# A diffusion backbone on one core: a new issue order for its state-space layer, and the discretisation's factor moved from B into the powers

## The chip, the core and the metric

The program runs on one core of a Trainium2 chip. The core has a matrix engine (TensorE, PE in the profile; PEld is its weight load), three engines for elementwise work (VectorE = DVE, ScalarE = ACT, GpSimd = POOL), a queue engine for transfers (SyncE = SP), and 16 DMA engines. Each engine takes its own instructions strictly in the order in which the program issues them, and waits on semaphores for the others. The metric is device time in microseconds; lower is better.

## The reference

Two layers over 256 latent tokens of width 2048. Layer 0 mixes tokens with a bidirectional diagonal state-space layer over 128 groups of 16 channels and 64 states, followed by a GLU; layer 1 mixes with a pooling mixer. Each layer ends with a gated convolutional FFN. Norms, shifts, scales and gates come from a conditioning vector through a large weight `ada_w`. The part that the change touches:

```python
def _s5_discretize(lam_re, lam_im, log_step, b_re, b_im):
    dt = exp(log_step)[:, None]
    mag = exp(lam_re * dt)
    abar_re, abar_im = mag * cos(lam_im * dt), mag * sin(lam_im * dt)
    nr, ni = abar_re - 1.0, abar_im
    den = lam_re * lam_re + lam_im * lam_im
    fr = (nr * lam_re + ni * lam_im) / den
    fi = (ni * lam_re - nr * lam_im) / den
    bbar_re = fr[..., None] * b_re - fi[..., None] * b_im
    bbar_im = fr[..., None] * b_im + fi[..., None] * b_re

# per direction: h[t] = abar * h[t-1] + bbar u[t], first over 256 context tokens,
# then over the 256 latent tokens; y = Re(C h) + D u, and out = GLU(gelu(y) @ glu_w)
```

## The kernel before

The first 405 us of the program are the state-space layer; the GLU, the FFNs and the pooling mixer follow. The layer's tokens are cut into chunks of 8; the work inside a chunk goes through matrices made of powers of abar times B and C, and what passes from chunk to chunk goes through a tree and a scan. The groups are handled in two halves h of 64 groups, and these in eight blocks b of 8 groups.

The order of all instructions of this layer is one string, ORDER (line 30). Every name in it stands for a function; most functions are generators, and each mention runs one step of one, `*n` runs n steps. A step is a handful of instructions on one or two engines. The names that matter below:

- d1, d2, d3: the discretisation (`disc1` to `disc3`, lines 450 to 483): exponent, sine and cosine, and the factor (bbar = factor times B), kept in `fr` in three combinations. pl and ph add the position table to the tokens; sc, sx and s2 give the norms' factors (squares on ScalarE, sums on TensorE).
- b0, b1, b2 (`bbar`, line 485): seven VectorE steps each that multiply B by the factor, complex times complex with three products. b0 and b1 cover 32 groups each of half 0 (512 elements per partition), b2 all 64 of half 1 (1024 elements). B lies in `Bb`, three parts: the difference or sum, real, imaginary.
- p0, p1 (`powers`, line 504): powers 1 to 8 of abar, with difference and sum. qb (`q_b`, line 526) copies powers 0 to 7 for the B side on ScalarE, one direction forward, one backward; qo copies powers 1 to 8 for the C side; qa squares the eighth for the tree.
- B, T, S of a block, as B13 for half 1, block 3: B (`b_ops`) is five VectorE steps of 1024 elements that form powers times B, with a small GpSimd-queue load `Cz`; T (`b_turn`) has three parts: two halves that TensorE transposes and ScalarE copies, and a third ("lg") of small products with C, copied to a lag table, on which GpSimd runs two small additions; S (`s_unit`) multiplies the tokens with the transposed result on TensorE and copies it to the chunk states on ScalarE.
- t0 to t3 (`tree`) and Z0, Z1 (`scan`, 31 steps) run on VectorE alone. t0 needs S00 to S03, t1 S04 to S07, Z0 both; t2, t3, Z1 likewise in half 1.
- c loads C of a block on the GpSimd queue; C (`c_ops`) forms C times powers on VectorE in three steps; M (`m_turn`) transposes the lag table; H (`hist`) copies the scan's states on ScalarE and adds on GpSimd; Y (`y_unit`) is the block's output on TensorE, and needs C, M and H. O (`y_out`) is gelu, transposition and a split into two 16-bit halves for four blocks.
- k (`columns`) takes the shift and scale of a quarter of the columns from `mod`, through TensorE and ScalarE, to `ck`; D (`modulate`), u, in form the normalised, modulated tokens on VectorE.
- F (`feed`, line 213) loads 1 MB of `ada_w` on the SP queue into one of the slots st and multiplies it on TensorE; when a part of the columns is full, the next F or N (`finish`) takes the sums through ScalarE, TensorE and ScalarE again, and a GpSimd addition puts them into `mod`. "-" and "+" take slot 2 away and give it back.
- lB, lc, lx, lt, le are loads for half 1 (lB on SP, the others on the GpSimd queue). W, h, l, G start the GLU: weights loaded, their 16-bit high part (ScalarE), low part (VectorE), and the first products.

Buffers are shared: the scratch G, cut into `e[0]` to `e[5]`, Z and WH carry in turn B's products, the transposed blocks and C's products (`o_view`, three buffers for eight blocks). B of block b+2 writes where T's third part of block b reads; C of block b+3 writes where Y of block b reads.

Of the kernel before, what the change touches and what calls it, by code (L numbers as in the profile page):

```python
# [7 lines left out]
OP = mybir.AluOpType  # L8
# [3 lines left out]
P = 128  # L12
# [3 lines left out]
HG = 64  # L16
# [11 lines left out]


ORDER = """  # L30
d1*17 d2*39 sc pl ph F sx F*2 d3 b0 p0 b0 p0 b0*3 p0*2 b0*2 qb0 B00*5 F*2 N F*4 d2 s2 u0*2 k0 qo0 - T00*2 B02 T00 u1*2
D000 D001 D000 D001 B01*5 b1*7 S00*2 B02*4 F*2 T01*3 qa0 F*2 T02*3 B03*5 F S01*2 B04*5 F T03 F*2 S02*2 N k1 c01 T03*2
D010 D011 D010 D011 B05 S03*2 c00 T04*2 B05*4 B06 F B06 T04 B06*3 F S04*2 t0*2 T05*3 B07*5 S05*2 c02 F C00*3 c03 T06*3
S06*2 T07*3 F S07 t0*2 S07 C01*3 c04 t0*6 F t1*10 Z0 C02 lB lc lt le C02 Z0 lx Z0 C02 Z0 F c05 Z0 b2 Z0*4 b2 F b2 F Z0
F b2 Z0 b2 Z0 F*2 b2 M00 b2 Z0 F Z0 p1 Z0 F p1 Z0 F M01 p1 in Z0 in Z0 M02 F in Z0*3 p1 Z0*8 F Z0*2 F qb1 qa1 H00 H01
Y00*2 M03 H02 F C03*3 c06 k2 Y01 c07 Y01 H03 M04 F*2 C04*3 N k3 D101 D111 D101 Y02*2 H04 C05*3 Y03*2 D100 O0 M05 H05
M06 F C06*3 O0 Y04*2 H06 M07 + C07*3 qo1 D100 Y05*2 F H07 O0 Y06*2 B10*5 Y07*2 O1 F B11*5 - T10*2 D111 T10 T11*3 B12*5
S10*2 O1*2 D110*2 B13*5 F S11 T12*3 B14*4 S12*2 F T13*3 B15*3 S11 B14 F T14*2 B15*2 F S13*2 c10 C10 F C10*2 T14 F B16
T15*3 B16*4 S14*2 c11 t2*2 B17*5 S15*2 c12 t2*6 F t2*2 c13 T16*3 S16*2 T17*3 S17*2 C11*3 c14 F C12 F*2 t3*4 F t3*5 t3
Z1 C12 Z1*2 F C12 Z1 c15 Z1*5 F Z1*2 M10 F Z1*4 M11 Z1 Z1 F Z1*2 M12 Z1*2 F Z1 F Z1*3 F*2 Z1*2 F Z1*4 H10 H11 Y10*2 H12  # L40
M13 C13*3 c16 Y11*2 H13 M14 Y12 F Y12 H14 M15 C14 C15*2 Y13 C15 Y13 C14*2 c17 O2 H15 M16 C16*2 F C16 Y14*2 H16 O2 M17 F
C17*3 Y15*2 F N W*3 H17 h O2 Y16*2 Y17*2 l O3*2 G O3
"""


class Net:
# [331 lines left out]
    def s5(self):  # L378
        tc, nc, A = self.tc, self.nc, self.A
        con, par = self.con, self.par  # L380
        with tc.tile_pool(name="s5c", bufs=1) as cp, tc.tile_pool(name="tb", bufs=2) as tb, tc.tile_pool(
# [63 lines left out]
            w = e[2][:, 0:1024].rearrange("p (v g) -> p v g", v=8)  # L445
# [20 lines left out]
            def disc3():  # L466
                self.mul(ab, ab, mg[:, None, :].to_broadcast([P, 2, NG]))
                nr, t1, t2 = w[:, 0], w[:, 1], w[:, 3]
                self.ts(nr, ab[:, 0], -1.0, OP.add)
                self.mul(t1, lr, lr)  # L470
                self.mul(t2, li, li)
                self.mul(w[:, 5], nr, lr)
                self.add(t1, t1, t2)
                self.mul(w[:, 6], ab[:, 1], li)
                nc.vector.reciprocal(w[:, 4], t1)
                self.mul(t1, ab[:, 1], lr)
                self.mul(t2, nr, li)
# [45 lines left out]

            pview = lambda mem: mem.rearrange("p (v k g) -> p v k g", v=4, k=8)

            def q_b(QB, pw):
                for lo, s in ((0, 7), (64, 0)):
                    nc.gpsimd.memset(QB[lo : lo + 64, 0, s], 0.0)
                    nc.gpsimd.memset(QB[lo : lo + 64, 1:3, s], 1.0)
                self.copy(QB[0:64, :, 0:7], pw[0:64, 1:4, 6::-1])  # L530
                self.copy(QB[64:128, :, 1:8], pw[64:128, 1:4, 0:7])

            def q_o(pw):
                self.copy(QO[0:64], pw[0:64, 1:4])
                self.copy(QO[64:128], pw[64:128, 1:4, ::-1])
# [261 lines left out]
            def st(v):  # L797
                sts[v] = stats((cx, xr)[v], v)

            ops = {  # L800
                "F": lambda: self.feed(1),
                "N": self.finish,
                "W": self.load,
                "h": lambda: self.high(0),
                "l": lambda: self.ensure(0),
                "G": self.glu0,
                "lB": lambda: nc.sync.dma_start(Bb[:, 1:3], A["b"][1]),
                "lc": lambda: nc.gpsimd.dma_start(rc, A["cck"][:, HG:, :]),
# [23 lines left out]
                ops[f"t{i}"] = lambda i=i: tree(32 * (i % 2), 32 * (i % 2) + 32)  # L832
            for h in range(2):
                ops[f"p{h}"] = lambda h=h: powers(h, pw[h])
                ops[f"qb{h}"] = lambda h=h: q_b(QB[h], pw[h])
                ops[f"qa{h}"] = lambda h=h: q_a(pw[h])
                ops[f"qo{h}"] = lambda h=h: q_o(pw[h])
                ops[f"Z{h}"] = scan
                for v in range(2):
                    for j in range(2):  # L840
                        ops[f"D{h}{j}{v}"] = lambda h=h, j=j, v=v: modulate(h, j, v)
                for b in range(8):
                    n = f"{h}{b}"
                    ops["B" + n] = lambda h=h, b=b: b_ops(h, b, QB[h], Bk[h][b], bm[h][b])
                    ops["T" + n] = lambda h=h, b=b: b_turn(h, b)
                    ops["S" + n] = lambda h=h, b=b: s_unit(h, b, bm[h][b])
                    ops["c" + n] = lambda h=h, b=b: c_load(h, b)
                    ops["C" + n] = lambda h=h, b=b: c_ops(h, b)
                    ops["M" + n] = lambda h=h, b=b: m_turn(h, b)
                    ops["H" + n] = lambda h=h, b=b: hist(b)  # L850
                    ops["Y" + n] = lambda h=h, b=b: y_unit(h, b)
            live = {}
            steps = (s.split("*") for s in ORDER.split())
            for tok in (s[0] for s in steps for _ in range(int(s[1]) if len(s) > 1 else 1)):
# [4 lines left out]
                r = ops[tok]()  # L859
# [601 lines left out]
```

## Time and profile before

| | us |
|---|---|
| median of 3 runs | 2081.57 (2080.56 to 2083.05) |
| profiled execution, device time | 2081.02 |
| its span, first to last instruction | 2079.2 |
| TensorE busy in the span | 1907.9 (92%) |
| VectorE busy | 1687.5 (81%) |
| ScalarE busy | 977.4 (47%) |
| GpSimd busy | 111.6 (5%) |

The page's strip of 40 equal slices shows two programs in one: in the first eight slices VectorE is at 7 to 9 tenths and TensorE goes up and down between 3 and 7; from the ninth slice on TensorE is at 9 tenths or more almost throughout, with one dip between the GLU and the first FFN and one at the pooling mixer. The page's chain of work that ended last reaches back only into the second part (PE 47% of the span), so the first part is read from the busy times by stage, the waits and the timelines. In those views a row of a wait names the waiting engine, what it wrote, and which engine ended the wait.

### The profile page before, as it was taken

The page shows a single profiled execution, that of the slowest core. Times are in us where ns is not written, and L with a number is a line of the kernel's source. Part 1 is how long each engine was busy: PE and PEld are TensorE (multiplying, and loading weights), DVE is VectorE, ACT ScalarE, POOL GpSimd, SP SyncE. Part 2 cuts the span into 40 slices and gives each one's busy share as a digit, 9 for nine tenths or more (in the row PEclk, how much of TensorE's full clock was granted, in tenths as well). Part 3 has the DMA queues.
Part 4 walks back from the last instruction along what each step waited for, and adds up shares of the span by engine and source line. Part 5 has one row for each costly group of instructions (what it writes and reads, how often), then busy time and mean ns, then how long its engine had stood idle before and what let it go on. Part 6 is the DMA issues. An engine that isn't in the chain of part 4 may idle for free. (4 is left out here: it accounts for less than half of the span.)

```text
span 2079.2 us, 44155 instructions
## 1 busy us (share of the span) xinstructions
PE 1907.9 (92%) x19300; PEld 1624.0 (78%) x19300; DVE 1687.5 (81%) x2204; ACT 977.4 (47%) x1139; POOL 111.6 (5%) x129
## 2 busy tenths in 40 slices
PE   5773775799989999999999999889999999999998
PEld 3651552688878888888888888578888888888886
DVE  8799889699889999999998898878777766654444
ACT  2341651655555554554444443655545555543442
POOL 0440251200000000000000000000000000000000
PEclk9785897899989999999999999889999999999999
DMA  8565347599938999999999999327767656555652
GB/s 320 223 237 215 138 179 264 217 356 367 334 111 335 340 355 341 333 338 328 343 332 357 358 366 353 137 100 264 259 236 261 242 201 203 198 190 201 209 201 77
DMA packets 77585, 541.62 MB, mean 260 GB/s; under 512 B 8912, under 2 KB 9168, under 8 KB 16464
## 3 DMA queue, kind: packets, MB, share of 16 engines
q1 hardware_dynamic: 74304, 526.06, 69.1%
q0 software_dynamic: 3088, 12.74, 1.6%
q8 instruction: 151, 2.47, 0.5%
q14 instruction: 42, 0.34, 0.0%
HBM read 536.67 MB, written 2.10 MB: 259 GB/s over the span
## 5 line engine op out<-in xcount | busy, mean ns | idle before, releaser
L82 PEld LDWEIGHTS <-WH 128*128 128x128 f16 x9472 | 927.3, 98 | 118.7 <-issue 9.5
L70 DVE SCALAR_TENSOR_TENSOR XW<-st,WH 128x2048 f16<-128x2048 f32 (+1 forms) x303 | 676.2, 2233 | 276.3 <-ACT WH L74 275.8
L74 ACT ACTIVATE WH<-st 128x2048 f16<-128x2048 f32 (+1 forms) x304 | 566.7, 1865 | 704.8 <-PE pu L82 364.4
L82 PE MATMUL pu<-Z,WH 128*128 128x256 f16 x5376 | 881.2, 273 | 0.0
L82 PE MATMUL pu<-Z,XW 128*128 128x256 f16 x2688 | 732.7, 273 | 0.0
L82 PEld LDWEIGHTS <-XW 128*128 128x128 f16 x4720 | 462.6, 98 | 59.6 <-issue 3.4
L82 PE MATMUL pd<-G,WH 128*128 128x256 f16 x2816 | 461.8, 273 | 0.2 <-DVE G L52 0.2
L82 PE MATMUL pd<-G,XW 128*128 128x256 f16 x1408 | 383.8, 273 | 0.0
L70 DVE SCALAR_TENSOR_TENSOR gac<-ra,cpad,gac 128x1024 f32<-128x1024 f32 x128 | 163.9, 1280 | 3.2 <-DMA ra<-ada 1.8
L82 PE MATMUL pg<-Z,WH 128*128 128x256 f16 x960 | 157.5, 273 | 0.0
L70 DVE SCALAR_TENSOR_TENSOR gac<-st,cpad,gac 128x1024 f32<-128x1024 f32 x112 | 143.4, 1281 | 7.3 <-DMA st<-ada 5.8
L70 DVE SCALAR_TENSOR_TENSOR hc<-pu,cvs,hc 128x255 f32<-128x255 f32 x336 | 138.6, 475 | 0.6 <-ACT hc L76 0.6
L82 PE MATMUL pg<-Z,XW 128*128 128x256 f16 x480 | 130.8, 273 | 1.6 <-DVE XW L70 1.6
L82 PE MATMUL gv<-st,cpad 128*32 128x128 f32 (+2 forms) x1024 | 87.7, 476 | 45.4 <-DMA st<-ada 45.4
L82 PEld LDWEIGHTS gv<-st,cpad 128*32 128x32 f32 x1024 | 30.9, 128 | 76.5 <-DMA st<-ada 60.7
L76 ACT ACTIVATE hc<-pu,par,cvs 128x256 f32<-128x256 f32 x168 | 84.3, 551 | 8.0 <-DVE G L52 8.0
L82 PE MATMUL y<-G,QX 128*32 128x128 f32 x768 | 32.0, 302 | 39.1 <-ACT QX L74 37.9
L82 PEld LDWEIGHTS y<-G,QX 128*32 128x32 f32 x768 | 23.9, 122 | 42.5 <-ACT QX L74 39.4
L52 DVE TENSOR_TENSOR G<-G,q 128x768 f32<-128x768 f32 (+2 forms) x56 | 49.8, 890 | 5.5 <-ACT q L74 3.6
L74 ACT ACTIVATE QX<-XW 64x512 f32<-64x512 f32 x32 | 35.7, 1116 | 36.3 <-DVE XW L52 30.3
L82 PE MATMUL pf<-Z,WH 128*128 128x256 f16 x256 | 47.7, 291 | 5.4 <-ACT Z L74 3.2
L74 ACT ACTIVATE hc<-hc 128x256 f32<-128x256 f32 x88 | 35.6, 405 | 27.7 <-DVE hc L70 26.4
(231 smaller groups left out, 1511.9 us busy)
## 6 DMA issues: line engine op xcount, KB each, us to landing
st<-up SPq DMA_DIRECT2D x176, 1024.0 KB, 6.2
st<-ada SPq DMA_DIRECT2D x128, 1024.0 KB, 6.8
ra<-ada SPq DMA_DIRECT2D x64, 1024.0 KB, 7.2
st<-down SPq DMA_DIRECT2D x64, 1024.0 KB, 5.1
st<-glu SPq DMA_DIRECT2D x32, 1024.0 KB, 7.5
st<-down SPq DMA_DIRECT2D x32, 768.0 KB, 5.3
Cz<-cz POOLq DMA_DIRECT2D x16, 256.0 KB, 5.3
G<-pool SPq DMA_DIRECT2D x4, 1024.0 KB, 8.5
```

Of the source, the lines that this page charges most:

```text
L52: self.nc.vector.tensor_tensor(out=out, in0=a, in1=b, op=op)
L70: self.nc.vector.scalar_tensor_tensor(out, a, s, b, op0, op1)
L74: self.nc.scalar.activation(out, a, f, scale=scale)
L76: self.nc.scalar.activation(out, a, f, bias=bias, scale=scale)
L82: self.nc.tensor.matmul(out, l, r, start=start, stop=stop)
```

## The change

Three functions change, and the order string is replaced as a whole.

- `bbar` becomes `bdiff`, one step: only the difference of B's parts is formed, without the factor.
- A new function `fpowers` (names f0, f1, seven steps each) multiplies powers 1 to 7 by the factor, 448 elements per step and partition; power 0 times the factor is a ScalarE copy of `fr`. Its result lies in QO for half 0 and in QX for half 1.
- `q_b` copies that result whole, 1536 elements for 1344, and its four GpSimd memsets per half go. `disc3` forms the three combinations of the factor with other signs, again in three instructions.

```diff
-d1*17 d2*39 sc pl ph F sx F*2 d3 b0 p0 b0 p0 b0*3 p0*2 b0*2 qb0 B00*5 F*2 N F*4 d2 s2 u0*2 k0 qo0 - T00*2 B02 T00 u1*2
-D000 D001 D000 D001 B01*5 b1*7 S00*2 B02*4 F*2 T01*3 qa0 F*2 T02*3 B03*5 F S01*2 B04*5 F T03 F*2 S02*2 N k1 c01 T03*2
-D010 D011 D010 D011 B05 S03*2 c00 T04*2 B05*4 B06 F B06 T04 B06*3 F S04*2 t0*2 T05*3 B07*5 S05*2 c02 F C00*3 c03 T06*3
-S06*2 T07*3 F S07 t0*2 S07 C01*3 c04 t0*6 F t1*10 Z0 C02 lB lc lt le C02 Z0 lx Z0 C02 Z0 F c05 Z0 b2 Z0*4 b2 F b2 F Z0
-F b2 Z0 b2 Z0 F*2 b2 M00 b2 Z0 F Z0 p1 Z0 F p1 Z0 F M01 p1 in Z0 in Z0 M02 F in Z0*3 p1 Z0*8 F Z0*2 F qb1 qa1 H00 H01
-Y00*2 M03 H02 F C03*3 c06 k2 Y01 c07 Y01 H03 M04 F*2 C04*3 N k3 D101 D111 D101 Y02*2 H04 C05*3 Y03*2 D100 O0 M05 H05
-M06 F C06*3 O0 Y04*2 H06 M07 + C07*3 qo1 D100 Y05*2 F H07 O0 Y06*2 B10*5 Y07*2 O1 F B11*5 - T10*2 D111 T10 T11*3 B12*5
-S10*2 O1*2 D110*2 B13*5 F S11 T12*3 B14*4 S12*2 F T13*3 B15*3 S11 B14 F T14*2 B15*2 F S13*2 c10 C10 F C10*2 T14 F B16
-T15*3 B16*4 S14*2 c11 t2*2 B17*5 S15*2 c12 t2*6 F t2*2 c13 T16*3 S16*2 T17*3 S17*2 C11*3 c14 F C12 F*2 t3*4 F t3*5 t3
-Z1 C12 Z1*2 F C12 Z1 c15 Z1*5 F Z1*2 M10 F Z1*4 M11 Z1 Z1 F Z1*2 M12 Z1*2 F Z1 F Z1*3 F*2 Z1*2 F Z1*4 H10 H11 Y10*2 H12
-M13 C13*3 c16 Y11*2 H13 M14 Y12 F Y12 H14 M15 C14 C15*2 Y13 C15 Y13 C14*2 c17 O2 H15 M16 C16*2 F C16 Y14*2 H16 O2 M17 F
-C17*3 Y15*2 F N W*3 H17 h O2 Y16*2 Y17*2 l O3*2 G O3
+d1 sc d1*2 lt d1*12 c00 d1*2 d2*8 c01 d2*17 c03 d2*2 pl d2*8 ph sx d3 p0 F*2 b1 p0 b0 p0*2 f0*7 qb0 qo0 s2 F*3 N B00*2
+u1 B01*2 B00*3 F B01 u0 B01*2 T00*2 F T01 u1 F*2 - T00 B02 T01*2 qa0 k0 d2 F*2 u0 B02*4 T02 D001 D000 T02*2 D001 D000
+S01*2 S00 B03*4 S00 B03 T03 B04*3 F T03*2 S02 F B05*4 S02 B05 B04*2 S03*2 F T04*2 F T04 B06*3 T05 B06*2 t0*2 T06 F*2 N
+T05*2 B07*3 t0 B07*2 k1 T07 t0 T07 d2 C00 D011 F D010 D011 T06 D010 S04*2 C00 t0*2 S07 lB d2 b2 t0*2 p1 S07 C00 p1*2
+t0 S06*2 lc p1 f1*4 S05 t0 S05 f1 t1*8 d2 F*2 M03 M00 c02 F*3 t1*2 Z0 T07 Z0*8 f1 F Z0*3 F*2 f1 qb1 Z0*10 M02 Z0 le
+M01 Z0 lx F Z0*4 M04 Z0 F Z0*2 T06 F*3 C01*3 H00 Y00 C02 c04 H01 Y00 H02 F Y01*2 H03 C03 C02*2 Y02 C03 in c05 Y02
+C04*3 F H04 M05 C03 Y03*2 F in O0 k2 c07 C05 c06 in C05*2 D101 H05 M07 F C06*2 Y04 C06 Y04 C07*2 c11 H06 M06 Y05*2 B10
+F*2 B10*3 O0 Y06*2 H07 N k3 C07 qo1 D100 Y07 O0 F B10 T10 D101 Y07 D100 O1 qa1 T10 + F T10 B11*4 D110 S10*2 O1 B11 F
+O1 B12*4 T11 - F B12 T11*2 S11*2 B13*5 T12 F D110 T12*2 T13 B14*3 S12*2 B14*2 T13 D111 F T13 B15*2 S13 B15*2 S13 T14 F
+T14*2 B15 T15*2 D111 B16*3 F B16*2 T15 S15 S14 B17*5 t2 S15 t2*7 S14 F t2*2 T16 F T16 T17*2 S16*2 S17*2 t3*7 F t3 F
+t3*2 M12 Z1*13 M14 F Z1 F*2 Z1*4 M13 c12 Z1*3 F Z1*4 F*2 T17 Z1 M11 Z1 F*3 Z1*4 M10 c10 C10*3 C11*3 T16 C12*2 d2 F*2
+C12 H10 Y10*2 H11 c13 c14 F H12 M15 c15 Y11 F Y11 H13 M16 Y12*2 H14 M17 C13*3 Y13*2 c16 C14*3 C15*3 C16*3 O2 F*2 W*3
+c17 Y14*2 H15 N C17 Y15*2 H16 Y16*2 C17*2 H17 Y17*2 h O3 O2 l O2 O3 G O3
@@ disc3
-                self.mul(fr[:, 0], t1, w[:, 4])
-                self.sub(fr[:, 1], w[:, 5], fr[:, 0])
-                self.stt(fr[:, 2], w[:, 5], -1.0, fr[:, 0], OP.mult, OP.subtract)
+                self.stt(fr[:, 0], t1, -1.0, w[:, 4], OP.mult, OP.mult)
+                self.add(fr[:, 1], fr[:, 0], w[:, 5])
+                self.sub(fr[:, 2], fr[:, 0], w[:, 5])
@@ bbar becomes bdiff; fpowers is new
-                self.sub(b[:, 0], b[:, 1], b[:, 2])
-                self.mul(v(1), v(1), f(1))
-                self.mul(v(2), v(2), f(2))
-                self.mul(v(0), v(0), f(0))
-                self.add(b[:, 1], b[:, 1], b[:, 0])
-                self.sub(b[:, 2], b[:, 2], b[:, 0])
-                self.add(b[:, 0], b[:, 1], b[:, 2])
+                self.sub(b[:, 0], b[:, 2], b[:, 1])
+            def fpowers(h, pw, pf):
+                m, p = pf[:, :, 1:8], pw[:, :, 0:7]
+                f = lambda r: fr[:, r, h * HG : (h + 1) * HG][:, None, :].to_broadcast([P, 7, HG])
+                self.copy(pf[:, :, 0], fr[:, :, h * HG : (h + 1) * HG])
+                self.mul(m[:, 2], p[:, 2], f(0))
+                self.mul(m[:, 1], p[:, 0], f(1))
+                self.mul(m[:, 0], p[:, 1], f(2))
+                self.sub(m[:, 1], m[:, 1], m[:, 2])
+                self.add(m[:, 0], m[:, 0], m[:, 2])
+                self.sub(m[:, 2], m[:, 0], m[:, 1])
+                self.add(m[:, 1], m[:, 0], m[:, 1])
@@ q_b
-                for lo, s in ((0, 7), (64, 0)):
-                    nc.gpsimd.memset(QB[lo : lo + 64, 0, s], 0.0)
-                    nc.gpsimd.memset(QB[lo : lo + 64, 1:3, s], 1.0)
-                self.copy(QB[0:64, :, 0:7], pw[0:64, 1:4, 6::-1])
-                self.copy(QB[64:128, :, 1:8], pw[64:128, 1:4, 0:7])
+                self.copy(QB[0:64], pf[0:64, :, ::-1])
+                self.copy(QB[64:128], pf[64:128])
```

A mention of a step that has already run out, as the five late d2, does nothing.

## Rows read from the trace of the kernel before

**Rows 1.** Stretches: PE, PEld, DVE, ACT, POOL busy (count), PE clock, DMA share, GB/s

```profile
0.00:155.10 155.10, 105.42 (x1900) 78.03 (x1900) 133.69 (x268) 52.98 (x70) 50.12 (x54) 0.85 0.69 261
...
369.00:403.10 34.10, 28.66 (x601) 22.54 (x602) 23.54 (x21) 28.33 (x27) 10.96 (x17) 0.91 0.42 159
403.10:555.00 151.90, 150.22 (x1380) 133.11 (x1378) 138.80 (x110) 82.66 (x99) 0.00 (x0) 1.00 0.95 363
```

**Rows 2.** TensorE's timeline: start, us, line, operation, shape, count [idle before, releaser]

```profile
276.76 1.06 PE L82 MATMUL gv<-st,cpad 128*32 128x512 f32 x8
278.90 1.09 PE L592 MATMUL pb<-con,Z 128*128 128x128 f32 x8 [1.07 <-ACT XW L74]
...
283.31 1.16 PE L82 MATMUL lg<-Z,Cz 64*32 64x128 f32 x64 [1.11 <-ACT G L74]
...
289.98 2.08 PE L82 MATMUL pS<-Y,G 128*64 128x64 f32 x64
...
403.08 0.38 PE L82 MATMUL pg_sm<-Z,WH 128*128 128x256 f16 x2
```

**Rows 3.** Waits of VectorE, 7 to 405.6 us: total us, times, longest us

```profile
DVE Y L52 <- ACT ck L74: 10.4, 3, 8.0
DVE G L52 <- PE y L82: 10.3, 4, 4.4
DVE G L70 <- ACT WH L74: 4.6, 1, 4.6
DVE gsc L70 <- POOL mod L262: 3.2, 1, 3.2
DVE cd L52 <- DMA cb<-c: 2.4, 1, 2.4
DVE Z L52 <- PE lg L82: 2.0, 1, 2.0
DVE Z L52 <- ACT Z L74: 1.6, 2, 0.8
DVE G L52 <- ACT QX L74: 1.5, 1, 1.5
```

**Rows 4.** VectorE's timeline: first step, D010, C04, C13, first weight split, last step

```profile
6.38 0.49 DVE L67 TENSOR_SCALAR G<-G 128x128 f32<-128x128 f32 x2 [1.56 <-DMA G<-lam]
...
104.53 4.65 DVE L52 TENSOR_TENSOR Y<-Y,ck 128x1024 f32<-128x1024 f32 x4 [8.00 <-ACT ck L74]
...
222.37 2.36 DVE L52 TENSOR_TENSOR G<-cb,QO 128x1024 f32<-128x1024 f32 x2 [3.34 <-PE y L82]
...
373.43 2.72 DVE L52 TENSOR_TENSOR G<-cb,QO 128x1024 f32<-128x1024 f32 x2 [4.45 <-PE y L82]
...
401.22 2.29 DVE L70 SCALAR_TENSOR_TENSOR G<-st,WH 128x2048 f16<-128x2048 f32 x1 [4.62 <-ACT WH L74]
404.34 1.23 DVE L52 TENSOR_TENSOR Z<-pz,Z 128x1024 f16<-128x1024 f32 x1 [0.83 <-ACT Z L74]
```

**Rows 5.** VectorE's groups by shape, 0 to 410 us: count, busy us, mean ns

```profile
L52 DVE TENSOR_TENSOR WH<-WH 128x512 f32<-128x512 f32 x8 | 5.4, 689 | 0.1
...
L52 DVE TENSOR_TENSOR WH<-WH 128x1024 f32<-128x1024 f32 x4 | 4.9, 1219 | 0.0
...
L52 DVE TENSOR_TENSOR WH<-WH,fr 128x512 f32<-128x512 f32 x6 | 3.9, 690 | 0.0
L52 DVE TENSOR_TENSOR WH<-WH,fr 128x1024 f32<-128x1024 f32 x3 | 3.6, 1218 | 0.0
...
L52 DVE TENSOR_TENSOR pt<-G 128x256 f32<-128x256 f32 x2 | 0.8, 418 | 0.0
```

**Rows 6.** ScalarE's group for the copy at the end of S, 0 to 410 us

```profile
L74 ACT ACTIVATE XW<-pS 128x1008 f32<-128x1008 f32 x16 | 31.4, 1975 | 34.5 <-PE pS L82 34.5
```

**Rows 7.** GpSimd's timeline, one addition to mod

```profile
82.61 10.39 POOL L262 TENSOR_TENSOR mod<-pcs,par 128x8 f32<-128x8 f32 x1 [1.82 <-ACT pcs L74]
```

**Rows 8.** DMA issues, 0 to 405 us: count, KB each, median us to landing

```profile
Cz<-cz POOLq DMA_DIRECT2D x16, 256.0 KB, 5.3
```

More of the change, by code (lines that the diff above doesn't have):

```diff
@@ L480, in disc3, with bdiff @@
                 self.mul(w[:, 5], w[:, 5], w[:, 4])
-                self.mul(fr[:, 0], t1, w[:, 4])
-                self.sub(fr[:, 1], w[:, 5], fr[:, 0])
-                self.stt(fr[:, 2], w[:, 5], -1.0, fr[:, 0], OP.mult, OP.subtract)
-            def bbar(h, g0, g1):
+                self.stt(fr[:, 0], t1, -1.0, w[:, 4], OP.mult, OP.mult)
+                self.add(fr[:, 1], fr[:, 0], w[:, 5])
+                self.sub(fr[:, 2], fr[:, 0], w[:, 5])
+            def bdiff(g0, g1):
                 b = Bb[:, :, g0 * 16 : g1 * 16]
-                v = lambda r: b[:, r].rearrange("p (g c) -> p g c", c=16)
-                f = lambda r: fr[:, r, h * HG + g0 : h * HG + g1][:, :, None].to_broadcast([P, g1 - g0, 16])
-                self.sub(b[:, 0], b[:, 1], b[:, 2])
+                self.sub(b[:, 0], b[:, 2], b[:, 1])
[4 more added lines that the diff above has]
+                self.mul(m[:, 2], p[:, 2], f(0))
                 yield 1
-                self.mul(v(1), v(1), f(1))
+                self.mul(m[:, 1], p[:, 0], f(1))
                 yield 1
-                self.mul(v(2), v(2), f(2))
+                self.mul(m[:, 0], p[:, 1], f(2))
                 yield 1
-                self.mul(v(0), v(0), f(0))
+                self.sub(m[:, 1], m[:, 1], m[:, 2])
                 yield 1
-                self.add(b[:, 1], b[:, 1], b[:, 0])
+                self.add(m[:, 0], m[:, 0], m[:, 2])
                 yield 1
-                self.sub(b[:, 2], b[:, 2], b[:, 0])
+                self.sub(m[:, 2], m[:, 0], m[:, 1])
                 yield 1
-                self.add(b[:, 0], b[:, 1], b[:, 2])
+                self.add(m[:, 1], m[:, 0], m[:, 1])
             def powers(h, pw):
@@ L524, in s5, with q_b @@
             pview = lambda mem: mem.rearrange("p (v k g) -> p v k g", v=4, k=8)
-            def q_b(QB, pw):
-                for lo, s in ((0, 7), (64, 0)):
-                    nc.gpsimd.memset(QB[lo : lo + 64, 0, s], 0.0)
-                    nc.gpsimd.memset(QB[lo : lo + 64, 1:3, s], 1.0)
-                self.copy(QB[0:64, :, 0:7], pw[0:64, 1:4, 6::-1])
-                self.copy(QB[64:128, :, 1:8], pw[64:128, 1:4, 0:7])
+            def q_b(QB, pf):
+                self.copy(QB[0:64], pf[0:64, :, ::-1])
+                self.copy(QB[64:128], pf[64:128])
             def q_o(pw):
@@ L791, in s5 @@
             pw = [pview(e[3]), pview(Z[1])]
+            pf = [QO, QX]
             QB = [QX, QY]
@@ L822, in s5 @@
                 "in": inputs,
-                "b0": lambda: bbar(0, 0, 32),
-                "b1": lambda: bbar(0, 32, 64),
-                "b2": lambda: bbar(1, 0, 64),
+                "b0": lambda: bdiff(0, 32),
+                "b1": lambda: bdiff(32, 64),
+                "b2": lambda: bdiff(0, 64),
                 "-": lambda: self.slots.remove(2),
@@ L834, in s5 @@
                 ops[f"p{h}"] = lambda h=h: powers(h, pw[h])
-                ops[f"qb{h}"] = lambda h=h: q_b(QB[h], pw[h])
+                ops[f"f{h}"] = lambda h=h: fpowers(h, pw[h], pf[h])
+                ops[f"qb{h}"] = lambda h=h: q_b(QB[h], pf[h])
                 ops[f"qa{h}"] = lambda h=h: q_a(pw[h])
```

## Prediction

> **What bounds the kernel now.** I read the busy times by stage first [rows 1]. From 403.1 to 555 us TensorE is busy 150.22 of 151.9 us at clock 1.00: from its first GLU product on, the program is TensorE's, so the state-space layer matters only through the moment at which that product can start, 403.08 [rows 2]. Ahead of it VectorE is the fullest engine (133.69 of 155.1 us in the first stretch), and TensorE, ScalarE and GpSimd run ahead of it until they need one of its results. Its instructions stand one behind the other from 6.4 us (first step of d1) to 405.6 (last step of O3) [rows 4], 399.2 us. The next view is what VectorE waited for in that stretch [rows 3]: eight kinds, 36.0 us together, so 363.2 us are work and hand-offs. A new order can only touch the 36.0; new arithmetic only the 363.2. Third, the timeline says where the waits lie: 8.00 us at D010 right behind k1, 3.34 at C04 and 4.45 at C13 behind the two scans, 4.62 at the first weight split [rows 4]. The first three have one cause: the VectorE step that needs a result of TensorE or ScalarE is issued too close behind the step that gives them their input.
>
> **Arithmetic.** bbar over B's 16 columns goes: eight and six steps over 512 elements, four and three over 1024, 5.4 + 3.9 + 4.9 + 3.6 = 17.8 us [rows 5]. Added: bdiff, two steps at 689 ns and one at 1219, 2.6 us; fpowers twice, seven steps over 448 elements each. No row has 448; 256 elements take 418 ns and 512 take 689 [rows 5], which gives 621 by the straight line between them, 14 x 0.62 = 8.7 us. The ends, 418 and 689, give 5.9 and 9.6. In d3 three small steps become three others: nothing. Net 17.8 - 2.6 - 8.7 = **6.5 us less** VectorE work (5.6 to 9.3), all of it in the serial stream. ScalarE gets two small copies and longer q_b copies (1536 elements for 1344), GpSimd loses eight memsets. q_b now waits for f0, but s2 with its fourteen small steps stands between qb0 and B00 and covers the two ScalarE copies; where it doesn't, B00 waits as now, 1.5 us [rows 3].
>
> **The order.** I go through the new string and ask at each VectorE step that needs another engine how much VectorE work lies between it and what feeds it, against the price of that round trip. A B is five steps of 1.2 us, about 5.7 with their overlap; a C 3.6; modulate 1.2 a step. Each gap's value is an estimate with its ends.
>
> Start: lt, c00, c01 and c03 go to the front of GpSimd's queue, 0.6 MB beside the first loads; pl may come up to 1 us late. The first F stands behind sx, so its slot comes free, and the fourth ada transfer starts, later; the ninth F feeds k0. Behind k0 stand a step of u0 and four of B02, 5.7 us, before D001; the same kind of trip cost 8.0 of waiting with nothing between [rows 4]. 2.5 us (0 to 9).
>
> B04 rewrites e4, which S00 still reads: S01 and S00 take TensorE 2 x 2.1 us [rows 2], B03 covers 5.7. 1 us (0 to 2).
>
> k1 and D011: T07, a tree step and a step of C00 come between, 4.2 us; the part's finish stands 6.9 us ahead of k1. The 3.2 for the addition [rows 3] and the 8.0 go; 0.5 us stays (0 to 5).
>
> p1 rewrites Z1 behind half of S07, and t1 needs S04, S07, S06, S05, four ScalarE copies of 1.98 us and products of 2.1 [rows 2, 6]. They overlap to about 2.1 each, 11 us from D010, and 15 us of VectorE work lie between. 1 us (0 to 3). lB moves from the first scan to ahead of p1; the transfers behind it on SP wait for B07's last read, which delays ada pieces that nobody needs then.
>
> Behind the first scan: C01 and a step of C02 (4.9 us) stand before C03, which needs Y00 and so H00 behind the scan. T06 and T07 give their third part inside the scan; nothing on TensorE there depends on it, so they and the F's beside them run ahead. k2 has 5.9 us before D101. Of the 3.34 at C04, a wait at C03 and one at D that the sums hold as well [rows 3], 6.1 us, remains 1.5 (0 to 8).
>
> B10 overwrites what Y05 reads: 1 us (0 to 2).
>
> B13 to B17 each overwrite what the third part of T of two steps earlier reads. From one such read to the next TensorE does S (2.08), two transposing halves (1.09 each), a third part (1.16) and an F (1.06) [rows 2], 6.5 us; VectorE needs five B steps and mostly one of D, 6.9. There are four of these near-ties; now one costs 2.0 [rows 3], and T13 loses 1.1 us at each hand-off [rows 2]. 4 us (0 to 8).
>
> t3 behind S17, and the cb loads: 1 us (0 to 3).
>
> Behind the second scan C10, C11 and C12 now lie where VectorE stood 4.45 us, so H10 and Y10 are hidden. ScalarE has 28.33 us of work there [rows 1], fewer of them M's now, and VectorE's tail grows by three C to be the longer one. c16 is loaded behind H14's GpSimd add, and l waits for h and its weights. The waits there now are 4.45 and 1.5 for y, 4.62 and 0.83 [rows 3, 4], 11.4 us; 4.5 remain (2 to 7). Small waits that I can't place: 1.5.
>
> Sum of waits: 2.5 + 1 + 0.5 + 1 + 1.5 + 1 + 4 + 1 + 4.5 + 1.5 = **18.5 us** for 36.0, so 17.5 less. The four scans and trees keep their work, both orders hold 64 F, so the vector-matrix products left for the later layers are the same; slot 2 comes and goes around two F in both and is never taken.
>
> The profiled execution took 2081.02 us for a span of 2079.2; the median of the runs shown is 0.5 above it. 2081.0 - 6.5 - 17.5 = **2057.0 us**. Its own range: waits of 9 to 30 us give 2048 to 2069.
>
> **A rule against it.** A GpSimd addition of eight elements took 10.39 us while VectorE ran two whole B and part of the next stretch without a gap [rows 7]; its result is what k1 waits for. A fuller VectorE leaves fewer gaps. The Trainium skill, SBUF — State Buffer, section "Who interferes with whom", says that a VectorE instruction with two SBUF inputs and a GpSimd instruction that reads SBUF exclude each other for a whole instruction. By that rule the addition would wait some 1.2 us, one VectorE instruction, and the sum stands; the row shows nearly ten of them, so the trace is worse than the rule.
>
> **Rivals.** (1) *GpSimd starves.* Were the additions that feed k0, k1 and k2 each 10.39 us, the first would come some 9 us late, k1's 5 and k2's 8, where I count 4 for the three places: 18 more, 2075. For it: the row [rows 7]; against it: of the four k now only one waited for its addition, 3.2 us [rows 3]. Part of it, half, gives 2066. (2) *Only the arithmetic tells*, the waits going to other places at the old total: 2081.0 - 6.5 = 2074.5. For it: in a chain of in-order queues a removed wait shows the next. Against it: three of the largest four have clear cover now. (3) *Slower: the Cz loop.* Cz of B(b+2) is issued on GpSimd behind T b's two additions, lands 5.3 us later [rows 8], feeds T(b+2)'s third part (1.16), which must be done before B(b+4). With additions of 1.2 us, one VectorE step, the loop is 1.2 + 2.4 + 5.3 = 8.9 us for two B, 4.5 for one, hidden by 6.9. If each addition takes 10.39, it is 1.2 + 20.8 + 5.3 = 27.3 for two, 13.6 for one, 6.7 over the cover; the change turns slower once four of the sixteen B suffer so (24.0 / 6.7), and with eight the time is 2057 + 54 = 2111. (4) *The change does nothing*: VectorE isn't what the first GLU product waits for, but weights or ScalarE: 2081. Against it: ScalarE's busy 28.33 of 34.1 us.
>
> **How the numbers follow.** Forecast 0.68, GpSimd starves 0.13, arithmetic only 0.08, nothing 0.06, slower 0.05. A measurement of this kernel can tell 0.2%, 4.2 us, from no change, so faster is under 2077.4: 0.68 + 0.13 + 0.08 = 0.89, same 0.06, slower 0.05. The range takes the forecast's ends, a little more below for waits I doubt, and reaches to rivals 1 and 2: 2045 to 2075.
>
> **What would show it.** The first GLU product at about 379 us; VectorE's waits to there under 30 us, none of 8 at D; fpowers' steps near 0.62 us, and no step of WH with fr; C13 without 4 us in front. It is wrong if a wait over 5 us stands at k0, D001 or k2 with a long GpSimd addition before it, if B13 to B17 wait more than 8 us for the third parts, or if the first GLU product doesn't move with VectorE's end.

## The result, and the profile after

The changed kernel takes 2047.7 us (2045.82 to 2049.7, 4 runs) beside 2081.98 (2080.56 to 2083.05) for the kernel before on the same chip: ratio 0.9835, 95% interval 0.9822 to 0.9847. It is faster by 34.3 us; the forecast was 24 less than the profiled 2081.0, so 2057.0, with a range of 2045 to 2075.

The profiled execution, the slowest of the four, took 2049.7 us for a span of 2047.9, 31.3 less than before. TensorE's timeline of the kernel after (start, us, line, operation, shape, count) has the first GLU product at 372.57, against 403.08 [rows 2]:

```profile
372.57 0.38 PE L83 MATMUL pg_sm<-Z,WH 128*128 128x256 f16 x2
```

30.5 of the 31.3 us are won ahead of this product; behind it the span has 1675.3 us left, 1676.1 before. (Lines of helpers stand one lower than before, L53 for L52.) VectorE's busy time from its first step to that product parts the gain in two. Stretches of before, then of after (PE, PEld, DVE, ACT, POOL busy, clock, DMA share, GB/s):

```profile
6.30:403.08 396.78, 266.90 (x4640) 182.56 (x4641) 354.72 (x723) 156.92 (x185) 109.04 (x117) 0.81 0.58 217
```

```profile
8.60:372.57 363.97, 264.38 (x4640) 183.74 (x4641) 348.31 (x718) 158.48 (x187) 93.52 (x110) 0.85 0.64 237
```

VectorE's work fell from 354.72 to 348.31, 6.4 us; what it stood idle in the stretch from 42.06 to 15.66 (396.78 - 354.72 and 363.97 - 348.31), 26.4 us. The stretch began 2.3 us later, so 32.8 - 2.3 = 30.5. The waits of VectorE from 9 to 376 us after, which answer to [rows 3] (total us, times, longest us):

```profile
DVE Y L53 <- ACT ck L75: 3.4, 2, 2.0
DVE G L53 <- PE y L83: 2.6, 1, 2.6
DVE Z L53 <- ACT Z L75: 1.4, 1, 1.4
DVE G L53 <- PE pS L83: 1.2, 1, 1.2
DVE XW L71 <- ACT WH L75: 0.6, 1, 0.6
```

That is 9.2 us for 36.0. VectorE's timeline after at the places of [rows 4]: first step, D behind k0, B04, D011 behind k1, B10, the last step of O3 (idle before and its releaser in brackets):

```profile
8.62 0.49 DVE L68 TENSOR_SCALAR G<-G 128x128 f32<-128x128 f32 x2 [4.11 <-DMA G<-lam]
...
74.72 4.63 DVE L53 TENSOR_TENSOR Y<-Y,ck 128x1024 f32<-128x1024 f32 x4 [2.03 <-ACT ck L75]
86.27 6.90 DVE L53 TENSOR_TENSOR G<-QX,WH 128x1024 f32<-128x1024 f32 x6 [1.25 <-PE pS L83]
119.44 4.63 DVE L53 TENSOR_TENSOR Y<-Y,ck 128x1024 f32<-128x1024 f32 x4 [1.41 <-ACT ck L75]
...
220.66 3.50 DVE L53 TENSOR_TENSOR G<-st,WH 128x1024 f32<-128x1024 f32 x3 [2.64 <-PE y L83]
...
372.63 2.43 DVE L53 TENSOR_TENSOR Z<-pz,Z 128x1024 f16<-128x1024 f32 x2 [1.36 <-ACT Z L75]
```

None of the waits of 8.00, 3.34, 4.45 and 4.62 is there any more; the largest is a new one, at B10. The last stretch shows VectorE full where it was busy 23.54 of 34.1 us [rows 1]; after:

```profile
337.00:372.57 35.57, 27.75 (x584) 20.66 (x585) 34.27 (x32) 25.49 (x24) 14.95 (x20) 0.92 0.50 179
```

### The profile page after: what moved, and what is told of

It is laid out like the page before. It is cut to its first block, busy times and chain, and to the rows that moved or that the text cites. A ratio compares the mean times of both kernels' runs of the same rounds, so it can differ in the third digit from the quotient of the medians.

```text
span 2047.9 us, 44139 instructions
## 1 busy us (share of the span) xinstructions
PE 1905.8 (93%) x19300; PEld 1626.1 (79%) x19300; DVE 1682.1 (82%) x2200; ACT 979.0 (48%) x1141; POOL 97.1 (5%) x121
## 5 line engine op out<-in xcount | busy, mean ns | idle before, releaser
L53 DVE TENSOR_TENSOR G<-G,q 128x768 f32<-128x768 f32 (+2 forms) x56 | 49.8, 890 | 5.5 <-ACT q L75 3.6
L75 ACT ACTIVATE QX<-XW 64x512 f32<-64x512 f32 x32 | 35.7, 1116 | 25.1 <-DVE XW L53 16.7
```

Of the source, the lines that this page charges most:

```text
L53: self.nc.vector.tensor_tensor(out=out, in0=a, in1=b, op=op)
L75: self.nc.scalar.activation(out, a, f, scale=scale)
```

## The experiments

The theory at the start was the prediction's: the arithmetic takes some 6 us out of a serial VectorE stream, and the order takes waits away by putting VectorE work between a step and what feeds it. The main rival: a wait ends when another engine's queue says so, and work taken out or put in ahead of it leaves its end where it is.

**One half of the change at a time.** The old order with the new arithmetic:

```diff
-... F sx F*2 d3 b0 p0 b0 p0 b0*3 p0*2 b0*2 qb0 B00*5 ...
+... F sx F*2 d3 b0 p0*4 f0*7 qb0 B00*5 ...
 (likewise b1*7 becomes b1, the seven b2 one step, and f1*7 stands behind p1)
```

> The old order string with the new arithmetic: bdiff in one step where b0, b1 and b2 stood, f0 ahead of qb0 and f1 behind p1 in the first scan. Theory (the stage ends with VectorE's work plus its waits, both one to one): 5.9 to 6.5 us less VectorE work, but f0 now stands right ahead of qb0 with only the old B00 wait behind it, so B00's wait of 1.5 grows to about 2; the other waits stay. 2082.0 - 6 = 2076 us (2073 to 2078). Rival (a removed piece of work shows up as a wait, because other engines pace the stage): within 2 us of before, 2080 to 2082.

Measured: 2081.0 us, ratio 0.9993 [0.9982, 1.0005]: nothing. The stretch says that the work did go:

```profile
7.70:405.40 397.70, 270.25 (x4641) 185.39 (x4642) 349.18 (x719) 158.20 (x187) 99.24 (x113) 0.81 0.58 217
```

VectorE's 354.72 became 349.18, and its idle time 42.06 became 48.52. 5.5 us of work turned into 6.5 of waiting. Ahead of D010 went 3.6 of the 5.5 us, yet D010 starts 98.07 us behind the start of this stretch, 98.23 before: all of it came back as waiting, the largest part at D010 itself, 11.16 us for 8.00. The other 1.9 us went behind D010, where C04 waits 4.62 us for 3.34 and the rest is spread. VectorE's timeline and TensorE's ahead of D010, same kernel:

```profile
105.77 4.65 DVE L52 TENSOR_TENSOR Y<-Y,ck 128x1024 f32<-128x1024 f32 x4 [11.16 <-ACT ck L74]
```

```profile
97.92 1.93 PE L82 MATMUL gv<-st,cpad 128*32 128x256 f32 x16 [4.34 <-DMA st<-ada]
99.79 3.68 PE L82 MATMUL pS<-Y,Z 128*64 128x64 f32 x64
103.40 2.02 PE L82 MATMUL pk<-gsc,G 128*128 128x16 f32 x16
```

k1's product pk stands on TensorE behind an ada piece that was not there yet and behind half of S02. It ends at 105.42 and D010 starts 0.35 us later, however early VectorE was ready. At D010 the rival held.

The new order with the old arithmetic:

```diff
-... b1 p0 b0 p0*2 f0*7 qb0 ...
+... b1*7 p0 b0*7 p0*2 qb0 ...
 (likewise b2*7, and f1 is gone)
```

> The new order string with the old arithmetic: seven bbar steps where b0, b1 and b2 stand, no f0 and f1. Theory: the waits fall from 36 to about 9 us, the start is 2.2 us later as in the changed kernel, the work stays: 2082.0 - 27 + 2 = 2055 us (2051 to 2059), VectorE's waits behind d1 9 to 14 us. With the arithmetic alone the two parts add up to the whole change, -34. Rival (the order only works with the shorter B work): 2062 us or more.

Measured: 2057.69 us, ratio 0.9886 [0.9868, 0.9905], 23 us faster than before. Its stretch:

```profile
8.00:382.00 374.00, 272.86 (x4640) 190.20 (x4641) 356.85 (x722) 157.19 (x185) 106.31 (x114) 0.81 0.63 231
```

Idle time 17.15 us, nearly the 15.66 of the full change. So the order takes the waits and the arithmetic the work, but the parts don't add: the arithmetic is worth 0 on the old order and about 10 us on the new one, where little waiting is left that could take it back. Of these 10, VectorE's busy time has 8.5 (356.85 to 348.31): the 6.4 of the instructions and some 2 us of steps that are longer in this kernel. Most of these 2 are C's last product, `G<-cd,QO`, of 1414 ns on average here, 1316 after and 1217 before: it takes 1.75 us instead of 1.21 when a GpSimd addition runs beside it.

**k1 and D010.** The new arithmetic on the old order, with k1 taken out from behind what delayed it:

```diff
-... T03 F*2 S02*2 N k1 c01 T03*2 D010 ...
+... T03 F N k1 S02*2 F c01 T03*2 D010 ...
```

> The old order with the new arithmetic, and k1 issued one ada piece and two halves of S02 earlier on TensorE, so that pk of k1 no longer stands behind the gv product that waited 4.34 us for its ada transfer. Theory (the 6 us saved ahead of D010 turned into waiting because that ada piece in TensorE's queue sets when k1 can end): D010 starts at 100 to 101 us for 105.8, the waits for k1 and D010 fall by 4 to 6 us, and the first GLU product and the time by 4 to 5, to about 2076. Rival (another wait of the same chain stands right behind, or S02, now later, takes it): D010 or the steps behind it lose what is won, 2079 to 2082.

Measured: 2086.66 us beside 2084.39 for the kernel before, ratio 1.0007 [0.9995, 1.0020]: nothing, so the rival again. pk no longer had anything in front, and D010 still started at 105.85. GpSimd's timeline, TensorE's and VectorE's:

```profile
68.45 9.23 POOL L618 TENSOR_TENSOR st<-st,dm 128x16 f32<-128x16 f32 x2 [10.82 <-ACT dm L74]
```

```profile
81.86 1.96 PE L82 MATMUL lg<-G,Cz 64*32 64x128 f32 x64 [7.04 <-DMA Cz<-cz]
...
98.85 1.08 PE L82 MATMUL gv<-st,cpad 128*32 128x128 f32 x32 [1.01 <-DMA st<-ada]
...
101.94 3.56 PE L82 MATMUL pk<-gsc,G 128*128 128x16 f32 x16 [1.17 <-DVE gsc L65]
```

```profile
105.85 4.63 DVE L52 TENSOR_TENSOR Y<-Y,ck 128x1024 f32<-128x1024 f32 x4 [4.06 <-ACT ck L74]
...
150.79 2.36 DVE L52 TENSOR_TENSOR tr<-WH,XW 128x1024 f32<-128x1024 f32 x2 [4.51 <-ACT XW L74]
```

In this execution the additions of T01 were held for 9.23 us, Cz came late, TensorE stood 7.04 us at a third part, and the last ada piece of k1's quarter was late with it, so that VectorE waited 7.52 us for the addition ahead of k1 (3.15 before). And a new wait of 4.51 came at the second tree, which I put down to S02, now behind k1. So the ada piece and S02 are one cause of D010's place among several; this run does not single them out. What holds in all fourteen profiles is the 0.35 us (0.34 to 0.36). pk in before, in before once more, and after:

```profile
102.22 1.96 PE L82 MATMUL pk<-gsc,G 128*128 128x16 f32 x16
```

```profile
102.84 1.96 PE L82 MATMUL pk<-gsc,G 128*128 128x16 f32 x16
```

```profile
115.52 3.57 PE L83 MATMUL pk<-gsc,G 128*128 128x16 f32 x16 [4.45 <-DVE gsc L66]
```

They end at 104.18, 104.80 and 119.09, and D starts at 104.53 [rows 4], 105.15 and 119.44. In the new order pk starts 0.14 us behind its input (the last gsc ends at 115.38): TensorE has nothing else queued there.

The new kernel with k1 brought close to D011 tests whether it is the distance that removed the wait:

```diff
-... B07*2 k1 T07 t0 T07 d2 C00 D011 ...
+... B07*2 T07 t0 T07 d2 C00 k1 D011 ...
```

> The new kernel with k1 moved from ahead of two T07 steps, a tree step and a step of C00 to right ahead of D011, with one step of C00 between. Theory (distance between k1 and D011 is what removed the wait): D011 waits 4 to 6 us instead of 0.8 to 1.4, and the time rises by 3 to 5, to 2051 to 2053. Rival (the rows behind, S04 to S07 and the first tree, have slack that takes it back): within 1.5 us of the new kernel.

Measured: 2047.73 us, ratio 0.9831 [0.9812, 0.9851]: no change. VectorE's and TensorE's timeline:

```profile
117.84 4.63 DVE L53 TENSOR_TENSOR Y<-Y,ck 128x1024 f32<-128x1024 f32 x4 [2.42 <-ACT ck L75]
```

```profile
115.56 1.93 PE L83 MATMUL pk<-gsc,G 128*128 128x16 f32 x16 [1.34 <-DVE gsc L66]
```

With no VectorE work between (the step of C00 that the expectation names stands ahead of k1), the whole trip from k1 to D011 is 2.42 us, not 8. The distance was not what removed the wait: D011 waits 2.42 us for 1.41, not the 4 to 6 expected. What the timelines show in its place is a TensorE queue without a late ada piece in it; no run puts such a piece back into the new order. A shorter pk gives part back: 1.93 us here, 3.57 after. The stretches round pk, first after, then this kernel, show it with the granted clock:

```profile
111.00:115.50 4.50, 0.07 (x5) 0.01 (x1) 4.50 (x10) 0.55 (x4) 1.64 (x3) 0.84 0.66 211
115.50:119.10 3.60, 3.58 (x17) 3.60 (x18) 2.50 (x4) 0.00 (x0) 0.00 (x0) 0.50 0.94 396
```

```profile
111.00:115.50 4.50, 3.20 (x82) 2.62 (x80) 4.38 (x10) 3.47 (x6) 1.83 (x4) 1.00 1.00 410
115.50:117.50 2.00, 1.94 (x20) 1.94 (x24) 0.00 (x0) 0.00 (x0) 0.00 (x0) 1.00 0.99 418
```

TensorE idled for 4.45 us ahead of pk in the one and ran pk at 0.50, the lower of its two levels (1.2 and 2.4 GHz); in the other it was busy 3.20 of 4.50 us and ran it at 1.00. The gap alone doesn't set the price: the new kernel run again idled the same 4.45 us and ran pk in 2.98 us, at 0.67 in its first 1.9 us; and the kernel with H05's addition on VectorE, below, had TensorE busy 1.16 of the 4.50 us ahead, idle 1.07 right before pk, and ran it in 3.56 at 0.50.

The kernel before with D of columns 1 moved behind B05 is the prediction's own idea alone, cover by VectorE work:

```diff
-... T03*2 D010 D011 D010 D011 B05 S03*2 c00 T04*2 B05*4 B06 ...
+... T03*2 B05 S03*2 c00 T04*2 B05*4 D010 D011 D010 D011 B06 ...
```

> The kernel before with one place of the order changed: the four D steps of columns 1 stand behind B05 (five steps and S03, T04 later) and no longer right behind k1. Theory: the 8.0 us at D010 goes, S04 follows D010 as now with B06 between; 2082.0 - 8 = 2074 us (2072 to 2077). Rival (a removed wait shows the next one): the GpSimd addition or S04 to t1 takes the time back, 2078 to 2082.

Measured: 2079.99 us, ratio 0.9986 [0.9977, 0.9996]: faster by 3 us by the ratio (1 to 5), by 0.8 between the medians (2080.81 for the kernel before). D010's row in VectorE's timeline:

```profile
104.16 4.65 DVE L52 TENSOR_TENSOR Y<-Y,ck 128x1024 f32<-128x1024 f32 x4 [2.90 <-ACT ck L74]
```

D010 starts where it did, and B05 is done inside the wait. The wait fell by 5.1 us and that for the addition, 3.2 [rows 3], was gone, in part because VectorE's first step came 1.9 us later in this execution; y (10.3 to 12.0) and Z (1.6 to 2.6) took some back. Cover works, at less than half its face value of 8.

**The last stretch.** The new kernel with C10 to C12 ahead of the second scan, as before:

```diff
-... t3*2 M12 Z1*13 ... M10 c10 C10*3 C11*3 T16 C12*2 d2 F*2 C12 H10 ...
+... S17*2 c12 c10 ... t3*2 M12 T16 C10*3 C11*3 C12*3 Z1*13 ... M10 d2 F*2 H10 ...
```

> The changed kernel with one place undone: C10, C11 and C12 ahead of the second scan again, with their loads and T16's third part moved in front of them. Theory: VectorE stands in front of C13 for H10 and Y10 as in the kernel before, 4 to 5 us, and for the weights or y further on; the time is 4 to 9 us above the changed kernel's 2047.7, so 2052 to 2057. Rival (the tail is paced by ScalarE and TensorE, 25 to 28 us of work each in some 35): the wait appears but the first GLU product doesn't move, 2046 to 2050.

Measured: 2052.79 us, ratio 0.9864 [0.9847, 0.9880], 5 us more than after. The size is as expected, but by luck, since the wait is another one:

```profile
349.96 0.73 DVE L53 TENSOR_TENSOR cd<-cb 128x128 f32<-128x128 f32 x1 [7.60 <-DMA cb<-c]
```

C13 waits for its load, which GpSimd issues only behind H's additions (347.57), not for TensorE as in [rows 4]. So this run prices a late load, and not the place of the C steps.

The kernel before with these nine steps moved behind the second scan:

```diff
-... c10 C10 F C10*2 ... C11*3 c14 F C12 F*2 ... Z1 C12 Z1*2 F C12 ... Z1*4 H10 ...
+... c10 F ... F F*2 ... Z1*2 F ... Z1*4 C10*3 C11*3 C12*3 H10 ...
```

> The kernel before with its nine steps of C10, C11 and C12, and the loads they need, moved behind the second scan, as the new order has them; nothing else. Theory (the 4.45 us at C13 and the small waits in the last stretch were bought by doing these steps too early): the second scan ends about 10.8 us earlier, the rest to the first GLU product takes 2 to 4 us less than scan plus steps did before, waits there 11.4 to about 5, so 2073 to 2076. Rival (the loads on GpSimd's queue, or ScalarE's 28 us of work there, become the end of the stretch): 2078 to 2082.

Measured: 2088.7 us beside 2084.39, ratio 1.0029 [1.0013, 1.0044]: slower by 4 between the medians and 6 by the ratio, with the other sign than expected. VectorE's timeline, ScalarE's, and TensorE's last ada piece, here and then before:

```profile
324.21 2.36 DVE L52 TENSOR_TENSOR tr<-WH,XW 128x1024 f32<-128x1024 f32 x2 [4.19 <-ACT XW L74]
...
399.83 1.22 DVE L52 TENSOR_TENSOR Z<-pz,Z 128x1024 f16<-128x1024 f32 x1
408.31 2.29 DVE L70 SCALAR_TENSOR_TENSOR G<-st,WH 128x2048 f16<-128x2048 f32 x1 [7.26 <-ACT WH L74]
```

```profile
406.36 1.91 ACT L74 ACTIVATE WH<-st 128x2048 f16<-128x2048 f32 x1 [0.79 <-DMA st<-glu]
```

```profile
400.21 1.04 PE L82 MATMUL gv<-st,cpad 128*32 128x512 f32 x8
```

```profile
393.08 1.04 PE L82 MATMUL gv<-st,cpad 128*32 128x512 f32 x8
```

The 4.45 at C13 and 1.5 for y are gone as the theory said. But C11 had covered the copies of S17 at t3, which now cost 4.19; and the weight split waits for its weights. With the C steps later, Y and the last ada piece behind it came later on TensorE; the weights' load goes out right behind this piece (at 401.32, before at 394.18), so that VectorE waits 7.26 for the split, 4.62 before [rows 4]. These waits give and take nearly the same, within 1 us, and the profile agrees: its first GLU product comes 7.1 us later (410.17), but 5.0 of them lie ahead of the first moved step, where the order is the old one (B13's write at 289.28 for 284.30). Some 2 us are the edit's; the rest of the measured 4 to 6 the profile doesn't explain. The new order also moves two M (M13, M14) out of the tail into the scan and the weights ahead of Y14; ScalarE's half of the split is early there:

```profile
364.36 1.91 ACT L75 ACTIVATE WH<-st 128x2048 f16<-128x2048 f32 x1
```

VectorE's half starts at 368.99, without a wait. That the C steps pay only together with these is what I infer; it is not shown.

**What is left at B10 and at the start.** The new kernel once more, with the four early loads (lt, c00, c01, c03) behind the first two F, with H05's addition on VectorE, and with both:

```diff
-d1 sc d1*2 lt d1*12 c00 d1*2 d2*8 c01 d2*17 c03 d2*2 pl ... p0 F*2 b1
+d1 sc d1*16 d2*27 pl ... p0 F*2 lt c00 c01 c03 b1
-nc.gpsimd.tensor_tensor(out=Hs[:, :, 0], in0=Hs[:, :, 1], in1=Hs[:, :, 2], op=OP.add)
+(nc.vector if dve else nc.gpsimd).tensor_tensor(out=Hs[:, :, 0], in0=Hs[:, :, 1], in1=Hs[:, :, 2], op=OP.add)
```

> The changed kernel once more, as the measure for the next three on one chip. Its time should be 2047 to 2050 us. Its profile tells which waits are the order's and which are one execution's: the first step of d1 between 6.4 and 8.6 us as in the other profiles, waits at D00 and B04 that come and go with TensorE's own stalls, and the wait at B10 (2.6 us) if it belongs to the order.

> The changed kernel with lt, c00, c01 and c03 issued behind the first two F and no longer at the very start. Theory A (these 0.6 MB delay lam, the first load that VectorE needs): d1 starts some 2 us earlier than in the changed kernel and the time falls by 2, to 2046. Theory B (the start differs by execution: the old order in two other profiles started at 7.8 and 8.3 us without these loads): no change, within 1 us of the changed kernel.

> The changed kernel with one of the sixteen additions behind H, H05's, on VectorE (0.4 us) in the place of GpSimd, where it took 7.43 us while VectorE ran C without a gap and Y05 and then B10 waited. Theory: B10's wait of 2.6 us goes and 0.4 of work comes, 2045.5 to 2046.5, some 2 us under the changed kernel. Rival (Y05 is late for another reason, the long addition is an accident of the record): B10 still waits 2 us or more, no gain.

> Both edits of the two kernels before together: late lt, c00, c01, c03, and H05's addition on VectorE. Theory: the gains add, 0 to 4 us under the changed kernel, 2 by the second alone. Rival (a wait that goes is taken by the next, as it was in the old order with the new arithmetic): within 1 us of the changed kernel.

Measured beside 2080.23 for the kernel before: 2047.85 (0.9852 [0.9832, 0.9873]), 2048.37 (0.9847 [0.9833, 0.9861]), 2050.34 (0.9851 [0.9833, 0.9868]) and 2047.36 (0.9845 [0.9831, 0.9859]). None differs from the new kernel. The new kernel run again waited 8.9 us, 9.2 the first time. The loads do nothing: with them late, the first step's wait for `lam` was 2.6 us in one profile and 4.3 in the other. B10's wait comes from GpSimd. H05's addition after, in the new kernel run again, in the kernel with late loads (with the B10 row of VectorE behind it), and H06's with H05 on VectorE:

```profile
211.17 7.43 POOL L709 TENSOR_TENSOR QX<-QX 128x256 f32<-128x256 f32 x1 [8.71 <-ACT QX L75]
```

```profile
209.44 7.82 POOL L709 TENSOR_TENSOR QX<-QX 128x256 f32<-128x256 f32 x1 [9.47 <-ACT QX L75]
```

```profile
211.54 3.38 POOL L709 TENSOR_TENSOR QX<-QX 128x256 f32<-128x256 f32 x1 [11.64 <-ACT QX L75]
```

```profile
217.66 2.58 DVE L53 TENSOR_TENSOR G<-st,WH 128x1024 f32<-128x1024 f32 x2 [0.51 <-PE y L83]
```

```profile
217.52 5.96 POOL L709 TENSOR_TENSOR QX<-QX 128x256 f32<-128x256 f32 x1 [7.12 <-ACT QX L75]
```

7.43 us go with a wait of 2.64 at B10, and so do the 7.82 of the second execution and 7.85 in the kernel with early C, whose order is the same up to here: the wait belongs to the order. 3.38 go with 0.51, and 3.40 with 0.26 in the kernel with k1 close to D011; why these two let GpSimd in sooner is open. With H05 on VectorE the wait at B10 is gone, as expected, and the time does not fall. The hold passes to the next addition, and a wait of 3.15 for ScalarE's Z comes instead; with both edits that one doesn't come, and the time is the same again.

**The kernel before once more**, for a second profile:

> The kernel before once more, for a second profile of it. If the waits of the first profile belong to the order: D010 6 to 9 us, C13 4 to 5, C04 3 to 4, the first weight split 4 to 5, 33 to 39 together. The first step of d1 came at 6.4 us there and at 7.1 to 8.9 in the other profiles; if that belongs to the execution and not to the order, it comes here at 7 to 9.

Measured: 2081.43 us. D010 waited 6.10, the addition to `mod` 4.85, C04 4.37, C13 4.45, the first weight split 4.68; over the same stretch the waits are 35.7 us, 36.0 in the first profile. Only C04 lies outside what I expected (3 to 4). The waits belong to the order. The first step came at 7.15 us, 6.38 in the first profile and 7.1 to 8.9 in the others: that is the execution's. The addition of 10.39 us [rows 7]:

```profile
83.14 0.41 POOL L262 TENSOR_TENSOR mod<-pcs,par 128x8 f32<-128x8 f32 x1 [1.73 <-ACT pcs L74]
```

It took 0.41 us here, and D010 came at 105.15 for 104.53. The hold had cost nothing at D010.

## Why the prediction was right, and where it was not

**Place and sign.** Right: the gain lies ahead of the first GLU product, 30.5 of 31.3 us, and TensorE's part behind it kept its length. The product came at 372.57 where I looked for 379.

**Arithmetic.** The size was right: 6.5 us forecast, 6.4 less VectorE work. The steps of `fpowers`, for which I drew a line to 0.62 us, in VectorE's rows by tile (min/median/max ns):

```profile
L53 DVE TENSOR_TENSOR QO<-QO x4: 616/620/625, 41.1 to 42.9; 128x448 f32<-128x448 f32 x4
L53 DVE TENSOR_TENSOR QO<-G,fr x3: 616/617/617, 39.5 to 40.5; 128x448 f32<-128x448 f32 x3
```

The reason was not complete: "all of it in the serial stream" makes it sound as if less work were less time. On the old order it was worth nothing, on the new one about 10 us.

**Waits.** This is the term that was mis-sized: 18.5 us forecast, 9.2 measured. By place, forecast and then measured: D behind k0 2.5 and 2.0; B04 1 and 1.25; k1 and D011 0.5 and 1.4; p1 and t1 1 and none; behind the first scan 1.5 and none; B10 1 and 2.6; B13 to B17 4 and none; t3 and the cb loads 1 and none; the last stretch 4.5 and 1.9; small ones 1.5 and none.

- *B13 to B17* was the largest miss. I set 6.5 us of TensorE against 6.9 of VectorE as if a T began only when the whole B before it was done. TensorE's timeline after, and VectorE's:

```profile
240.25 1.06 PE L595 MATMUL pb<-con,Z 128*128 128x128 f32 x8 [0.47 <-DVE Z L53]
...
244.57 1.16 PE L83 MATMUL lg<-Z,Cz 64*32 64x128 f32 x64
```

```profile
238.89 1.21 DVE L53 TENSOR_TENSOR Z<-Z,G 128x1024 f32<-128x1024 f32 x1
...
241.16 1.21 DVE L53 TENSOR_TENSOR Z<-Z,G 128x1024 f32<-128x1024 f32 x1
...
250.29 2.35 DVE L53 TENSOR_TENSOR Z<-st,WH 128x1024 f32<-128x1024 f32 x2
```

  T11's first half starts when the step that ends at 240.10 is done; it needs only that part of B11, not the step of 241.16. Its third part is over at 245.73, and B13 writes there at 250.29. TensorE waits for VectorE in this stretch, not the other way round: this near-tie had 4.6 us of slack, and those at B15 and B17 3.6 and 4.6.
- *k0, k1.* The totals were near, the reason was wrong. I priced the trip from k to D at 8.0 and sought VectorE work to cover it; that a step issued too close behind its feeder was the one cause of the three waits does not hold here. The trip is 2.42 us; the rest was TensorE's queue. I also took the addition of 10.39 us for what k1 waits for; it was the next one, at 95.86, 0.20 us long, and that waited for TensorE too.
- *GpSimd starves*, the first rival, happened in small, at a place that I had not named: H05, 7.43 us, for 1.6 us more than forecast at B10. The Trainium skill, SBUF — State Buffer, section "Who interferes with whom", has a VectorE instruction with two SBUF inputs and a GpSimd instruction that reads SBUF exclude each other. By that rule the hold would be one VectorE instruction, an estimate of 1.2 us. The trace does not agree: the addition ended only when VectorE had fallen idle at 218.0, seven instructions later.
- *The last stretch.* I counted on the place of the C steps. By itself it gains nothing, as the kernel before with them moved shows. M and the weights, which I only counted as ScalarE's share, moved too; whether they are the other half no run shows.

**The rival "arithmetic only"** had its rule right, that a removed wait shows the next, and its object wrong: what fell to it was the arithmetic alone, not the order. The rivals "slower" and "does nothing" are out: no wait for a third part is left, and the first GLU product moved by 30.5 us with VectorE's end.

**Open.** That the order takes the waits away is shown, by the half of the change with the order alone; which placement takes which wait is not. Why the other placements of the order leave TensorE's queue free ahead of k1 is read from the timelines, not tried move by move; nor have I tried M and W alone in the last stretch. Nothing was tried on the wait at C04.

## What to carry to other kernels

Ask of each wait what sets its *end*: if it is another engine's queue (here TensorE's product pk, 0.35 us ahead of D in every profile), work taken out ahead of the wait becomes waiting, 3.6 us of it at D010. Price a round trip without what happened to be queued in it: 2.42 us, where the row showed a wait of 8.00. And don't add up moves that were tried alone: on the old order the arithmetic gave 0 us, the later D -3 and the later C 4 to 6 more; the whole new order gave -23 without the arithmetic and -34 with it.

## What was not expected of the hardware

- A GpSimd addition beside back-to-back VectorE steps took 0.41 or 10.39 us in two executions of one kernel. H05's took 7.43 to 7.85 in three executions whose order is the same up to there, and 3.38 and 3.40 in two kernels with something changed ahead.
- The other way round, a VectorE step of 1024 elements took 1.75 us for 1.21, and a pair of them 2.89 for 2.35, when a GpSimd addition ran beside it: seven times in the last stretch after.
- TensorE ran pk in 1.93 us at clock 1.00 and in 3.57 at 0.50, after 4.45 us of idling; after as long a gap in a second execution it took 2.98. A free queue has a price of 1.0 to 1.6 us here, just where the wait for it ends.
- The first VectorE step waited for its first load until 6.38 to 8.9 us, by execution, a range of 2.5 us beside a spread of 3.9 in the new kernel's times.
